# Value products of attention: high and low halves side by side in one stationary tile

## The chip, the cores and the metric

One core of one Trainium2 chip runs the kernel. The metric is device time in microseconds (us). The engines are named as in the profile: PE (TensorE matmul), PEld (its weight load), DVE (VectorE), ACT (ScalarE), POOL (GpSimd), SP (SyncE, which here only issues DMAs).

## The reference, cut to what matters

512 tokens of width 1024 pass through two layers of one block and then through a second block.

- Layer 1: short convolutions beside attention over a memory of 256 rows (4 heads of 64), then a feed-forward part.
- Layer 2: banded attention (12 query heads, 4 value heads of 64, each block of 128 tokens sees itself and the block before) beside memory attention, then a feed-forward part.
- Second block: eight heads of 64 in two groups. Each head adds three attentions, each with its own gate: over compressed blocks, over selected blocks and over a window. With 512 tokens the selected blocks are all the valid ones and the window holds all earlier tokens, so both of these are plain causal attention:

```
p = masked_softmax(q @ k.T * scale, causal)     # branch 0: k_s, v_s; branch 1: k_w, v_w
o = g_c * (p_c @ v_c) + g_s * (p_s @ v_s) + g_w * (p_w @ v_w)
flat = blocks of 32 tokens, stride 16;  k_c, v_c = gelu(flat @ w1) @ w2     # 31 blocks a group
```

Four retention heads, gates and an output projection follow.

## The kernel before, in words

All products are made at nearly full fp32 precision from pieces of a shorter type (`float32r`). A value x is split into hi = round(x) on ACT (`copy`, L65) and lo = x - hi on DVE (`lo_of`, L75, or L71 with a scale). A product is then three matmuls into the same PSUM tile: hi*hi, hi*lo, lo*hi (`mm3`, L111 to L113; `proj_tok`, L133 to L135). Weights come by DMA into `wr`, are split into `wh` and `wl`, and are used once.

In an attention the scores of 128 queries go into a PSUM tile `lg` (`logits`, L234 and L235), DVE subtracts mask and maximum, ACT makes the exponentials and their sum, DVE scales the rows. PE transposes the probabilities 128x128 at a time (L253) into a PSUM tile `tp`, and `split_p` splits these into hi (ACT) and lo (DVE). `pv` then multiplies by the values. A value tile holds, per key block, hi and lo of all heads with 64 zero columns between neighbours, so that a stationary of 128 columns is either [value, 0] or [0, value]. Both heads of a pair thus accumulate into one PSUM tile `po` of 128 rows: even head in rows 0 to 63, odd head in rows 64 to 127. The last key block has only 128 queries; `pv_last` copies these probabilities unsplit and does the product in full fp32 (L279). The compressed attention's product is full fp32 as well (L845).

Per pair of heads: memory attention (`mem_attention`) has 2 key blocks of 512 queries for each head; banded attention (`band_head`) has key blocks 0 to 2 of 256 queries and block 3 of 128; causal attention (`causal_head`, called for 2 branches) has key blocks 0 to 3 of 512, 384, 256 and 128 queries. There are 2 memory pairs in each of two layers, 6 banded pairs, and 4 causal pairs.

`compress` (called for keys and for values) makes flat (62 columns for 31 blocks of 2 groups) and multiplies it with four weight units of 4 x 256 columns, three matmuls of 256 columns for each of 16 pieces (L635 to L637).

Tiles come from pools with a fixed number of buffers for each tag; a tile waits until the buffer that it takes has been read for the last time. The dependences and the order on each engine are worked out when the kernel is built: code is taken in program order, and later work that is ready (projections of the next pair, the next stage) may be put ahead on an engine whose next work is not. Each engine then runs its own list in order. PSUM has `pp`=2, `lg`=3, `tp`=2, `po`=1 buffers of one bank. Probabilities live in `pa` (6 buffers of 512 columns): a causal head takes three, a banded head two.

Of the kernel before, what the change touches and what calls it, by code (L numbers as in the profile page):

```python
# [8 lines left out]
F32 = mybir.dt.float32  # L9
# [14 lines left out]
KWORDS = 2 * 9 * 64  # L24
# [3 lines left out]
class Build:  # L28
# [3 lines left out]
    def __init__(self, ctx, tc, T, out):  # L32
        self.tc, self.nc, self.T, self.out = tc, tc.nc, T, out
        pool = lambda n, b, **k: ctx.enter_context(tc.tile_pool(name=n, bufs=b, **k))
        self.cst = pool("cst", 1)
        self.wp = pool("wp", 1)
        self.wbufs = dict(wr=2, wh=3, wl=3)
        self.sl = pool("sl", 1)
        self.sm = pool("sm", 4)
        self.psp = pool("psp", 1, space=PSUM)  # L40
        self.dr = pool("dr", 1, space=DRAM)
        self.n = 0
        self.bufs = dict(h=16, b=16, t=4, pa=6, pb=10, q=4, v=4, x=8, R=1, s=3, sa=1, k3=2, v3=1)
        self.pbufs = dict(pp=2, lg=3, tp=2, po=1)
# [192 lines left out]
    def value_tile(self):  # L237
        v = self.slot("v", F32R, (128, KWORDS), "v")
        self.nc.gpsimd.memset(v.bitcast(F32), 0.0)
        return v.rearrange("p (s j c) -> p s j c", s=2, c=64)  # L240

    def fill_values(self, v, ps, rs):

        hi, lo = v[:, 0, 1::2], v[:, 1, 1::2]
        src = ps.rearrange("p (h c) -> p h c", c=64)
        self.copy(hi, src, rs)
        self.lo_of(lo, src, hi, rs)
# [20 lines left out]
    def last_value(self, ps, rs):  # L268

        v = self.slot("v3", F32, (128, 576), "v3").rearrange("p (j c) -> p j c", c=64)  # L270
        self.nc.gpsimd.memset(v, 0.0)
        self.copy(v[:, 1::2], ps.rearrange("p (h c) -> p h c", c=64), rs)
        return v

    def pv_last(self, po, v, kv, odd, ps, stop):
        t = self.slot("k3", F32, (128, 128), "k3")
        self.copy(t, ps)
        s = slice(2 * kv, 2 * kv + 2) if odd else slice(2 * kv + 1, 2 * kv + 3)
        self.nc.tensor.matmul(po, v[:, s].rearrange("p j c -> p (j c)"), t, start=False, stop=stop)  # L279
# [6 lines left out]
    def load_consts(self):  # L286
# [3 lines left out]
        self.const("pad", [128, 88])  # L290
        self.ones = self.const("ones", [128, 128])
        nc.vector.memset(self.ones, 1.0)
        self.zero = self.const("zero", [128, 128], F32R)
        self.copy(self.zero, self.ones, 0.0)
# [60 lines left out]
    def mem_kv(self, layer):  # L355
# [11 lines left out]
        def done(tb, ps):  # L367
            hl = [self.slot("b", F32R, name="mv")[:, :384] for _ in range(2)]
            for t in hl:
                nc.gpsimd.memset(t.bitcast(F32), 0.0)  # L370
            hi, lo = (t.rearrange("p (i c) -> p i c", i=2) for t in hl)
            for i in range(2):
                for o in range(2):
                    src = ps[:, 128 * i + 64 * o:128 * i + 64 * o + 64]
                    d = slice(128 * o, 128 * o + 64)
                    self.copy(hi[:, i, d], src, self.mrs[:, tb:tb + 1])
                    self.lo_of(lo[:, i, d], src, hi[:, i, d], self.mrs[:, tb:tb + 1])
            vs.append(hl)
# [4 lines left out]
    def mem_attention(self, qs, ks, vs):  # L383
# [3 lines left out]
        for pair in range(2):  # L387
            po = self.psum("po")
            for odd in range(2):
# [16 lines left out]
                for kb in range(2):  # L406
                    t = self.transposes([(qb * 128, ps_[qb][:, kb * 128:kb * 128 + 128]) for qb in range(4)], 512)
                    th, tl = self.split_p(t)
                    c = 192 * pair + 64 * odd
                    vh, vl = (x[:, c:c + 128] for x in vs[kb])  # L410
                    self.mm3(po, vh, vl, th, tl, odd == 0 and kb == 0, odd == 1 and kb == 1)
            res.append(self.split(po, "b", name="ym"))
# [93 lines left out]
    def layer_b(self):  # L506
# [17 lines left out]
        def done(tb, ps):  # L524
            v = self.value_tile()
            self.fill_values(v, ps, rs[:, tb:tb + 1])
            vs.append(v)
            if tb == 3:
                vs.append(self.last_value(ps, rs[:, 3:]))
# [8 lines left out]
        for pair in range(6):  # L538
            q = self.stack_q(self.queries(T["b_w_q"][pair], h, R))
            bias = self.bias(pair)  # L540
            po = self.psum("po")
            nc.tensor.matmul(po.rearrange("p (a b) -> p a b", a=4), self.zero, self.zero.unsqueeze(1).to_broadcast([128, 4, 128]), start=True, stop=False)
# [8 lines left out]
    def band_head(self, po, hd, odd, q, ks, vs, bias):  # L551
# [21 lines left out]
        cur, prev = (lambda kb: p[kb][:, -128:]), (lambda kb: p[kb + 1][:, :128])  # L573
        tp = self.transposes([(0, cur(0)), (128, prev(0)), (256, cur(1)), (384, prev(1))], 512)
        th, tl = self.split_p(tp)
        for kb in range(2):
            self.pv(po[:, kb * 128:kb * 128 + 256], vs[kb], kv, odd, th[:, kb * 256:kb * 256 + 256], tl[:, kb * 256:kb * 256 + 256], False, False)
        tp = self.transposes([(0, cur(2)), (128, prev(2)), (256, cur(3))], 384)
        th, tl = self.split_p(tp[:, :256])
        self.pv(po[:, 256:], vs[2], kv, odd, th, tl, False, False)  # L580
        self.pv_last(po[:, 384:], vs[4], kv, odd, tp[:, 256:384], odd == 1)
# [30 lines left out]
    def compress(self, kT, j):  # L612
# [14 lines left out]
        fs = [self.split(f.rearrange("p l c -> p (l c)"), "pb", n=496, name="fl") for f in fl]  # L627
        ps = self.psum("pp")[:62, :256]
        mm = nc.tensor.matmul
        for u in range(4):  # L630
            wh, wl = self.weights(T["cmp_w1"][j, u], 4, 256)
            for k in range(4):
                i = 4 * u + k
                a, b = (f[:, 62 * (i % 8):62 * (i % 8) + 62] for f in fs[i // 8])
                mm(ps, a, wh[:, k], start=i == 0, stop=False)  # L635
                mm(ps, b, wh[:, k], start=False, stop=False)
                mm(ps, a, wl[:, k], start=False, stop=i == 15)  # L637
        return ps

    def compress_gelu(self, ps, j):  # L640
# [4 lines left out]
        nc.vector.tensor_copy(x, ps)  # L645
# [30 lines left out]
    def compressed_v(self, hw):  # L676
# [4 lines left out]
        for g in range(2):  # L681
# [7 lines left out]
            for i in range(2):  # L689
                t = self.const(f"vc{g}{i}", [128, 128])  # L690
                nc.vector.memset(t, 0.0)
                for o in range(2):
                    r = slice(64 * i + 32 * o, 64 * i + 32 * o + 32)
                    nc.vector.tensor_copy(t[r, 64 * o:64 * o + 64], ps[r])
# [3 lines left out]
    def cmp_probs(self, g, qpair):  # L698
# [23 lines left out]
        t = self.slot("s", name="pct")  # L722
        self.copy(t, tp)
        return t

    def causal_head(self, po, hd, odd, branch, q, start):
        nc = self.nc
        g = hd // 4
        k = self.nk[branch][g]
        den, nm, r = (self.small(4, name=n) for n in ("den", "nm", "rec"))  # L730
        t = [self.slot("pa", name="p") for _ in range(3)]
        p = [t[0][:, :128], t[1][:, :256], t[0][:, 128:], t[2]]
        for qb in range(4):
            n = 128 * (qb + 1)
# [391 lines left out]
```

## Time and profile before

| | us |
|---|---|
| median of 3 runs | 1671.94 (1670.53 to 1672.93) |
| the profiled execution: its own time | 1670.48 |
| its span, first to last instruction | 1668.7 |
| PE busy | 1634.9 (98%) |
| PEld busy | 1374.2 (82%) |
| DVE busy | 1059.2 (63%) |
| ACT busy | 639.0 (38%) |
| POOL busy | 247.1 (15%) |

Busy time is the union of an engine's instructions. A matmul's row lasts until its result has landed, so rows of neighbouring matmuls overlap; the spacing of their starts is the time that one takes from PE. Parts of the span: memory attention of the first layer lies at about 70 to 100 us, that of the second at 605 to 640, banded attention at 630 to 705, compression at 1120 to 1205, causal attention at 1165 to 1330 us.

### The profile page before, as it was taken

The page shows a single profiled execution, that of the slowest core. Times are in us where ns is not written, and L with a number is a line of the kernel's source. Part 1 is how long each engine was busy: PE and PEld are TensorE (multiplying, and loading weights), DVE is VectorE, ACT ScalarE, POOL GpSimd, SP SyncE. Part 2 cuts the span into 40 slices and gives each one's busy share as a digit, 9 for nine tenths or more (in the row PEclk, how much of TensorE's full clock was granted, in tenths as well). Part 3 has the DMA queues.
Part 4 walks back from the last instruction along what each step waited for, and adds up shares of the span by engine and source line. Part 5 has one row for each costly group of instructions (what it writes and reads, how often), then busy time and mean ns, then how long its engine had stood idle before and what let it go on. Part 6 is the DMA issues. An engine that isn't in the chain of part 4 may idle for free.

```text
span 1668.7 us, 21221 instructions
## 1 busy us (share of the span) xinstructions
PE 1634.9 (98%) x8184; PEld 1374.2 (82%) x8184; DVE 1059.2 (63%) x1828; ACT 639.0 (38%) x1134; POOL 247.1 (15%) x220
## 2 busy tenths in 40 slices
PE   8999999999999999999999999998999999999997
PEld 6888888888888788888888888878788888888887
DVE  7776745444454979875434435588788977764443
ACT  5532333222333467633222223324465533333333
POOL 1111411002011600051100101351001000010010
PEclk9999999999999999999999999999999999999999
DMA  5323222322352422122332332332401122243342
GB/s 188 118 85 102 91 98 91 101 101 85 118 160 91 159 83 84 62 102 88 101 101 95 100 109 91 101 138 93 166 28 58 45 82 83 70 151 114 126 159 88
DMA packets 51557, 171.39 MB, mean 103 GB/s; under 512 B 6680, under 2 KB 6880, under 8 KB 51328
## 3 DMA queue, kind: packets, MB, share of 16 engines
q1 hardware_dynamic: 45504, 151.11, 27.3%
q0 software_dynamic: 5376, 18.82, 3.4%
q8 instruction: 64, 1.05, 0.2%
q14 instruction: 37, 0.30, 0.1%
q10 hardware_dynamic: 576, 0.11, 0.0%
HBM read 160.56 MB, written 11.81 MB: 103 GB/s over the span
## 4 chain that ended last, share of the span: by engine, by line
PE 82%; DVE 10%; issue 2%; ACT 2%; DMA 1%; POOL 1%; DVEq 0%; SPq 0%; ACTq 0%; POOLq 0%
PE pp L112 11%; PE pp L113 11%; PE pp L111 11%; PE lg L111 8%; PE lg L112 8%; PE lg L113 7%; PE tp L112 3%; PE tp L253 2%; PE tp L113 2%; PE tp L111 2%; DVE wl L75 2%; PE po L111 2%; PE po L112 2%; PE po L113 2%; PE pp L133 2%
## 5 line engine op out<-in xcount | busy, mean ns | idle before, releaser
L65 ACT ACTIVATE wh<-wr 128x1024 fp32r<-128x1024 f32 (+2 forms) x280 | 288.5, 1030 | 695.1 <-PE pp L112 228.0
L75 DVE TENSOR_TENSOR wl<-wr,wh 128x1024 fp32r<-128x1024 f32 (+2 forms) x280 | 388.7, 1389 | 55.5 <-ACT wh L65 52.3
L111 PE MATMUL pp<-gh,wh 128*128 128x512 f32 x880 | 348.0, 396 | 7.4 <-ACT wh L65 5.9
L113 PE MATMUL pp<-gh,wl 128*128 128x512 f32 x880 | 347.2, 395 | 0.6 <-DVE wl L75 0.6
L112 PE MATMUL pp<-gl,wh 128*128 128x512 f32 x880 | 346.7, 394 | 0.5 <-DVE gl L71 0.5
L111 PEld LDWEIGHTS pp<-gh,wh 128*128 128x128 f32 x880 | 166.7, 190 | 41.4 <-ACT wh L65 6.4
L113 PEld LDWEIGHTS pp<-gh,wl 128*128 128x128 f32 x880 | 166.4, 189 | 33.9 <-DVE wl L75 1.6
L112 PEld LDWEIGHTS pp<-gl,wh 128*128 128x128 f32 x880 | 166.6, 189 | 33.2 <-DVE gl L71 1.3
L111 PE MATMUL lg<-gh,wh 128*128 128x512 f32 x408 | 159.8, 392 | 0.0
L112 PE MATMUL lg<-gl,wh 128*128 128x512 f32 x408 | 159.1, 390 | 0.0
L113 PE MATMUL lg<-gh,wl 128*128 128x512 f32 x408 | 158.8, 389 | 0.0
L68 POOL TENSOR_TENSOR u<-u,z 128x512 f32<-128x512 f32 x44 | 64.8, 1472 | 549.7 <-DVE u L68 432.6
L68 DVE TENSOR_TENSOR u<-lg,Rf 128x512 f32<-128x512 f32 x44 | 30.4, 691 | 137.4 <-PE lg L113 137.3
L112 PEld LDWEIGHTS lg<-gl,wh 128*128 128x128 f32 x408 | 76.7, 188 | 16.5 <-issue 0.7
L111 PEld LDWEIGHTS lg<-gh,wh 128*128 128x128 f32 x408 | 76.6, 188 | 16.3 <-issue 0.5
L113 PEld LDWEIGHTS lg<-gh,wl 128*128 128x128 f32 x408 | 76.6, 188 | 16.1 <-issue 0.2
L112 PE MATMUL tp<-actl,wh 128*128 128x512 f32 x216 | 84.5, 391 | 0.9 <-DVE actl L75 0.9
L111 PE MATMUL tp<-acth,wh 128*128 128x512 f32 x216 | 84.1, 389 | 0.0
L113 PE MATMUL tp<-acth,wl 128*128 128x512 f32 x216 | 84.1, 389 | 0.0
L68 DVE TENSOR_TENSOR z<-pp,Rf 128x512 f32<-128x512 f32 x44 | 30.4, 691 | 69.5 <-PE pp L113 65.7
L504 DVE TENSOR_TENSOR x<-x,tp 128x512 f32<-128x512 f32 x36 | 24.6, 683 | 65.5 <-PE tp L113 65.5
L71 DVE SCALAR_TENSOR_TENSOR gl<-x,gains,gh 128x512 fp32r<-128x512 f32 x40 | 52.9, 1338 | 0.5 <-ACT gh L65 0.5
(422 smaller groups left out, 3088.9 us busy)
## 6 DMA issues: line engine op xcount, KB each, us to landing
wr<-in_w_gate_dram SPq DMA_DIRECT2D x44, 512.0 KB, 3.2
wr<-in_w_up_dram SPq DMA_DIRECT2D x44, 512.0 KB, 3.2
wr<-in_w_in_dram SPq DMA_DIRECT2D x44, 512.0 KB, 3.2
wr<-in_w_down_dram SPq DMA_DIRECT2D x32, 448.0 KB, 3.3
wr<-in_a_w_in_dram SPq DMA_DIRECT2D x18, 512.0 KB, 3.2
wr<-in_w_down_dram SPq DMA_DIRECT2D x16, 512.0 KB, 3.5
wr<-in_a_w_out_dram SPq DMA_DIRECT2D x8, 512.0 KB, 3.2
wr<-in_b_w_q_dram SPq DMA_DIRECT2D x8, 512.0 KB, 3.2
```

The costliest lines, as they stand in the source:

```text
L65: self.nc.scalar.activation(out, in_, AF.Copy, scale=scale)
L68: (eng or self.nc.vector).tensor_tensor(out, a, b, op=ALU.mult)
L71: (eng or self.nc.vector).scalar_tensor_tensor(out, a, s, b, op0=op0, op1=op1)
L75: self.nc.vector.tensor_tensor(out, x, hi.bitcast(F32), op=ALU.subtract)
L111: mm(ps, ah, bh, start=start, stop=False)
L112: mm(ps, ah, bl, start=False, stop=False)
L113: mm(ps, al, bh, start=False, stop=stop)
L133: mm(ps, a, wh, start=k == 0, stop=False)
L253: self.nc.tensor.transpose(ps[:, c:c + 128], src, self.ident)
L504: nc.vector.tensor_tensor(self.x[c], self.x[c], ps, op=ALU.add)
```

## The change

A value tile now holds, per head, 64 columns of hi and beside them 64 columns of lo, with no zeros; it is the stationary [hi | lo] of one matmul. The moving operand is the split probabilities: one pass with hi, one with lo, where there were three. The result has 128 rows for one head: rows 0 to 63 belong to hi of the values, 64 to 127 to lo, and `heads_out` adds the two halves (ACT copies the lower rows to SBUF, DVE adds) for each head of the pair. `po` becomes a tile of 1024 columns (two banks), and `lg` goes from three buffers to two.

- Memory attention: two matmuls of 512 columns in place of three for each head and key block.
- Banded attention: the softmax of both heads of a pair comes first (`band_probs`), then the products of both (`band_values`): two matmuls of 256 for each of 4 key blocks; the last block's 128 queries are padded with 128 zero columns (POOL). The matmul with zeros that opened `po` goes.
- Causal attention: both heads of a pair share keys and values, so their queries are put into one moving operand (`causal_pair`): 8 matmuls of 512 and 4 of 256 columns for a pair and a branch. Probabilities of a pair take five `pa` buffers. The branch is now the outer loop, the head the inner one.
- Compressed attention: four matmuls of 256 for each head, on split probabilities.
- Compression: flat's hi (62 columns) and lo (62 columns, from column 64) become one stationary, so two matmuls for each piece in place of three; `compress_gelu` adds the two halves.

```
-        self.bufs = dict(..., R=1, s=3, sa=1, k3=2, v3=1)
-        self.pbufs = dict(pp=2, lg=3, tp=2, po=1)
+        self.bufs = dict(..., R=1, s=4, sa=1)
+        self.pbufs = dict(pp=2, lg=2, tp=2, po=1)
...
-    def pv(self, po, v, kv, odd, th, tl, start, stop):
-        s = slice(2 * kv, 2 * kv + 2) if odd else slice(2 * kv + 1, 2 * kv + 3)
-        vh, vl = (v[:, i, s].rearrange("p j c -> p (j c)") for i in range(2))
-        self.mm3(po, vh, vl, th, tl, start, stop)
+    def pv(self, po, v, t, start, stop):
+        for i in range(2):
+            self.nc.tensor.matmul(po, v, t[i], start=start and i == 0, stop=stop and i == 1)
+    def heads_out(self, po, out, form=lambda a: a):
+        for o in range(2):
+            t = self.slot("s", name="half")[:64]
+            self.copy(form(t), po[o][64:])
+            self.nc.vector.tensor_tensor(form(out[64 * o:64 * o + 64]), po[o][:64], form(t), op=ALU.add)
...
 layer_b, for each pair:
-            for odd in range(2):
-                self.band_head(po, 2 * pair + odd, odd, q[odd], ks, vs, bias[:, odd])
-            ys.append(self.split(po, "b", name="y"))
+            probs = [self.band_probs(2 * pair + odd, q[odd], ks, bias[:, odd]) for odd in range(2)]
+            y = self.slot("t", name="yb")
+            po = self.band_values(pair, probs, vs)
+            self.heads_out([po[:, :512], po[:, 512:]], y)
+            ys.append(self.split(y, "b", name="y"))
...
+    def causal_pair(self, po, pair, branch, q):
+        mid = self.slot("pa", name="p")
+        for odd in range(2):
+            t = [self.slot("pa", name="p") for _ in range(2)]
+            p = [t[0][:, :128], mid[:, 256 * odd:256 * odd + 256], t[0][:, 128:], t[1]]
...            (scores, exponentials and scaling as in causal_head)
+        for kb, qbs in ((0, (0, 1)), (0, (2, 3)), (1, (2, 3)), (2, (2, 3))):
+            t = self.split_p(self.transposes(block(kb, qbs), 512))
+            self.pv(view[:, qbs[0] // 2], values[kb], [two(a) for a in t], branch == 0 and kb == 0, False)
+        t = self.split_p(self.transposes(block(1, (1,)) + [(256 + c, x) for c, x in block(3, (3,))], 512))
+        for i, kb in enumerate((1, 3)):
+            self.pv(view[:, i, :, 128:], values[kb], [two(a[:, 256 * i:256 * i + 256]) for a in t], False, False)
...
 compress:
-                mm(ps, a, wh[:, k], start=i == 0, stop=False)
-                mm(ps, b, wh[:, k], start=False, stop=False)
-                mm(ps, a, wl[:, k], start=False, stop=i == 15)
+                mm(ps, fs[u][:, k], wh[:, k], start=i == 0, stop=False)
+                mm(ps, fs[u][:, k], wl[:, k], start=False, stop=i == 15)
```

## Rows read from the trace of the kernel before

**Rows 1.** The page: engines' busy time; the chain that ended last.
```profile
PE 1634.9 (98%) x8184; PEld 1374.2 (82%) x8184; DVE 1059.2 (63%) x1828; ACT 639.0 (38%) x1134; POOL 247.1 (15%) x220
...
PE 82%; DVE 10%; issue 2%; ACT 2%; DMA 1%; POOL 1%; DVEq 0%; SPq 0%; ACTq 0%; POOLq 0%
```
**Rows 2.** Windows: stretch, length, busy us and instructions of each engine, clock, DMA.
```profile
core 0: us, PE busy (x) PEld busy (x) DVE busy (x) ACT busy (x) POOL busy (x), PEclk, DMA share, GB/s
60.00:80.00 20.00, 19.85 (x110) 17.18 (x110) 14.51 (x29) 12.88 (x31) 0.00 (x0) 0.97 0.32 107
80.00:100.00 20.00, 19.98 (x109) 16.35 (x108) 16.67 (x40) 11.77 (x35) 0.00 (x0) 1.00 0.29 93
...
620.00:640.00 20.00, 19.98 (x109) 16.23 (x107) 18.43 (x54) 14.61 (x42) 0.71 (x1) 1.00 0.13 41
640.00:660.00 20.00, 19.78 (x129) 17.07 (x128) 17.99 (x58) 14.26 (x42) 0.71 (x1) 1.00 0.28 93
660.00:680.00 20.00, 19.98 (x122) 16.80 (x121) 18.53 (x60) 15.18 (x46) 0.71 (x1) 1.00 0.24 70
680.00:700.00 20.00, 19.96 (x126) 16.96 (x126) 18.33 (x65) 14.50 (x47) 0.00 (x0) 1.00 0.22 76
...
1160.00:1180.00 20.00, 15.93 (x88) 13.64 (x89) 14.76 (x34) 12.04 (x22) 1.38 (x1) 0.91 0.47 153
...
1220.00:1240.00 20.00, 20.00 (x122) 16.95 (x121) 17.49 (x56) 13.34 (x37) 0.00 (x0) 1.00 0.00 1
1240.00:1260.00 20.00, 19.90 (x115) 16.87 (x114) 17.54 (x49) 11.71 (x33) 1.29 (x1) 1.00 0.15 53
1260.00:1280.00 20.00, 19.32 (x93) 15.10 (x93) 17.82 (x49) 11.99 (x31) 3.73 (x4) 1.00 0.21 67
1280.00:1300.00 20.00, 19.90 (x127) 17.09 (x126) 17.75 (x56) 12.10 (x36) 0.00 (x0) 1.00 0.09 27
1300.00:1320.00 20.00, 19.30 (x113) 15.92 (x112) 19.50 (x61) 14.62 (x42) 1.26 (x1) 1.00 0.01 2
```
**Rows 3.** Timeline of PE in causal attention: start, length, instruction.
```profile
1233.21 1.12 PE L845 MATMUL po<-pct,vc 128*128 128x512 f32 x2
1233.77 0.80 PE L235 MATMUL lg<-kl,q 128*128 128x512 f32 x1
...
1234.88 0.40 PE L111 MATMUL pp<-gh,wh 128*128 128x512 f32 x1
1235.11 0.39 PE L112 MATMUL pp<-gl,wh 128*128 128x512 f32 x1
```
**Rows 4.** Timeline in banded attention, at the end of one head's value products.
```profile
665.27 0.28 PE L113 MATMUL po<-tph,v 128*128 128x256 f32 x1
665.39 0.28 PE L111 MATMUL po<-tp,v 128*128 128x256 f32 x1
...
665.75 0.39 PE L279 MATMUL po<-k,v 128*128 128x128 f32 x2
665.89 0.48 PE L111 MATMUL pp<-gh,wh 128*128 128x512 f32 x1
```
**Rows 5.** Groups of DVE by shape, 600 to 712 us: busy, mean ns, idle before.
```profile
L75 DVE TENSOR_TENSOR tpl<-tp,tph 128x512 fp32r<-128x512 f32 x20 | 13.6, 687 | 1.9 <-ACT tph L65 1.8
...
L210 DVE TENSOR_TENSOR q<-qs,q 64x512 fp32r<-64x512 f32 x16 | 11.0, 686 | 0.8 <-ACT q L65 0.3
...
L75 DVE TENSOR_TENSOR tp<-tp,tp 128x256 fp32r<-128x256 f32 x12 | 5.0, 419 | 0.7 <-ACT tp L65 0.5
```
**Rows 6.** Groups of DVE by shape, 1205 to 1335 us.
```profile
L738 DVE CUSTOM_DVE_ANT_0 p<-lg,causal 128x512 f32<-128x512 f32 x14 | 9.5, 679 | 0.0
L75 DVE TENSOR_TENSOR tpl<-tp,tph 128x384 fp32r<-128x384 f32 x16 | 8.8, 548 | 1.0 <-ACT tph L65 0.9
```
**Rows 7.** Groups of ACT by shape, 1205 to 1335 us.
```profile
L739 ACT ACTIVATE p<-p,nm 128x512 f32<-128x512 f32 x14 | 10.0, 718 | 1.7 <-DVE nm L738 1.7
L65 ACT ACTIVATE tph<-tp 128x512 fp32r<-128x512 f32 x16 | 9.5, 592 | 9.7 <-PE tp L253 9.7
```
**Rows 8.** The chain that ended last, in compression alone (1140 to 1205 us).
```profile
by line: DVE wl L75 16.4%; PE pp L113 9.2%; PE pp L111 8.8%; PE pp L112 8.4%; DMA wr<-in_cmp_w_dram 7.6%; DVE flat L626 5.5%; DMA wr<-in_w_in_dram 5.4%; issue 4.1%; DVE kl L220 4.1%; ACT wh L65 3.3%; PE pp L637 2.6%; DVE v L71 2.5%; DVE rb 
```

More of the change, by code (lines that the diff above doesn't have):

```diff
@@ L23 @@
 WMAX = 1152
-KWORDS = 2 * 9 * 64
+KWORDS = 1024
 FFG = [(0, 8), (8, 15), (15, 22)]
@@ L367, in done @@
         def done(tb, ps):
[L368 to L378, printed above, removed]
+            vs.append(self.fill_values(ps, self.mrs[:, tb:tb + 1], "b"))
         self.proj_tok(T["w_mem_v"][layer], gm, 256, 2, done, tag=("tp",) if layer else ("lg",))
@@ L407, in mem_attention @@
                     t = self.transposes([(qb * 128, ps_[qb][:, kb * 128:kb * 128 + 128]) for qb in range(4)], 512)
[L408 to L412, printed above, removed]
+                    self.pv(po[:, 512 * odd:512 * odd + 512], vs[kb][:, h], self.split_p(t), kb == 0, kb == 1)
+            y = self.slot("t", name="ym")
+            self.heads_out([po[:, :512], po[:, 512:]], y)
+            res.append(self.split(y, "b", name="ym"))
         return res
@@ L688, in compressed_v @@
             two = []
[L689 to L694, printed above, removed]
+            for hd in range(4):
+                t = self.const(f"vc{g}{hd}", [128, 128], F32R)
+                nc.vector.memset(t.bitcast(F32), 0.0)
+                r = slice(32 * hd, 32 * hd + 32)
+                self.copy(t[r, :64], ps[r])
+                self.lo_of(t[r, 64:], ps[r], t[r, :64])
                 two.append(t)
@@ L721, in cmp_probs @@
         tp = self.transposes([(qb * 128, p[:, qb].rearrange("p h c -> p (h c)")) for qb in range(4)], 512)
[L722 to L726, printed above, removed]
+        return self.split(tp, "pb", name="pct")
+    def causal_pair(self, po, pair, branch, q):
         nc = self.nc
-        g = hd // 4
+        g = pair // 2
         k = self.nk[branch][g]
[L730 to L734, printed above, removed]
-            w = max(n, 256)
-            lg = self.psum("lg")
-            self.logits(lg[:, :w], q[:, qb * 128:qb * 128 + 128], [a[:, :w] for a in k])
-            nc.vector.tensor_tensor_reduce(p[qb], lg[:, :n], self.causal[:, 512 - n:], -1.0, 1.0e30, ALU.add, ALU.min, nm[:, qb:qb + 1])
-            nc.scalar.activation(p[qb], p[qb], AF.Exp, bias=nm[:, qb:qb + 1], scale=-1.0, accum_out=den[:, qb:qb + 1])
-        nc.vector.reciprocal(r, den)
-        self.mul(r, r, self.gates[:, :, hd * 3 + 1 + branch])
-        for qb in range(4):
-            self.scaled(p[qb], r[:, qb:qb + 1])
-        for kb in range(3):
-            parts = [((qb - kb) * 128, p[qb][:, kb * 128:kb * 128 + 128]) for qb in range(kb, 4)]
-            if kb == 2:
-                parts.append((512 - kb * 128, p[3][:, 384:]))
-            tp = self.transposes(parts, 0)
-            th, tl = self.split_p(tp[:, :512 - kb * 128])
-            self.pv(po[:, kb * 128:], self.nv[kb], 2 * branch + g, odd, th, tl, start and kb == 0, False)
-            if kb == 2:
-                self.pv_last(po[:, 384:], self.nv[4], 2 * branch + g, odd, tp[:, 512 - kb * 128:640 - kb * 128], False)
@@ new lines, in causal_pair @@
+        mid = self.slot("pa", name="p")
+        probs = []
+        for odd in range(2):
+            hd = 2 * pair + odd
+            den, nm, r = (self.small(4, name=n) for n in ("den", "nm", "rec"))
+            t = [self.slot("pa", name="p") for _ in range(2)]
+            p = [t[0][:, :128], mid[:, 256 * odd:256 * odd + 256], t[0][:, 128:], t[1]]
+            for qb in range(4):
+                n = 128 * (qb + 1)
+                w = max(n, 256)
+                lg = self.psum("lg")
+                self.logits(lg[:, :w], q[odd][:, qb * 128:qb * 128 + 128], [a[:, :w] for a in k])
+                nc.vector.tensor_tensor_reduce(p[qb], lg[:, :n], self.causal[:, 512 - n:], -1.0, 1.0e30, ALU.add, ALU.min, nm[:, qb:qb + 1])
+                nc.scalar.activation(p[qb], p[qb], AF.Exp, bias=nm[:, qb:qb + 1], scale=-1.0, accum_out=den[:, qb:qb + 1])
+            nc.vector.reciprocal(r, den)
+            self.mul(r, r, self.gates[:, :, hd * 3 + 1 + branch])
+            for qb in range(4):
+                self.scaled(p[qb], r[:, qb:qb + 1])
+            probs.append(p)
```

123 lines of the change are left out of this document (67 added, 56 removed).

## The prediction

> **What bounds the kernel now.** I read the page first. PE is busy for 98% of the span and carries 82% of the chain that ended last [rows 1]; DVE has 10% of the chain and 63% busy time. Taken alone this says that each PE microsecond removed is a microsecond of time. But a matmul's row runs on until its result has landed, so the busy share of PE cannot show how much room it has, and the share of DVE is an average over stages. So I read the windows of the stages that the change touches [rows 2]. The reader is to see two things there. In banded attention DVE is busy 18.43, 17.99, 18.53 and 18.33 us of 20: 73.3 of 80, 92%. In causal attention it is 17.49 to 19.50 of 20: 90.1 of 100. So in the two stages where most of the removed matmuls lie, a second engine is almost as full as PE. The fullest slice of all, 19.50 of 20, shows how far DVE can be packed in this kind of work: 97.5%. In memory attention of the first layer DVE has room (14.51 and 16.67 of 20). In compression even PE is not full (15.93 of 20, granted clock 0.91 of full speed), and the chain there is mostly the split of weights on DVE and the weights' DMAs [rows 8].
>
> The Trainium skill has a rule on just this (Perfetto Trace Analysis, Identifying the Most-Contended Engine): matmul busy time is no good measure of how near TensorE is to its limit, and the weight-load share should be read in its place, while for VectorE the busy share is fair. The windows agree as far as they go: by that rule banded attention has PE at 81 to 85% and DVE at 90 to 93%, so DVE is the most contended engine there, and the removal of matmuls by itself would give nothing in that stage. The sum below would stand without this rule.
>
> **What PE loses.** The cost of a matmul is the spacing of starts: 0.23 us for 512 columns (1234.88 to 1235.11) [rows 3], 0.12 us for 256 (665.27 to 665.39) and 0.14 us for the pair of records of one full fp32 product of 128 columns (665.75 to 665.89) [rows 4]. The full fp32 product of 512 columns takes 0.56 us (1233.21 to 1233.77) [rows 3]. For 384 columns I take the middle of 0.12 and 0.23, 0.175.
> - Memory attention: 2 layers x 2 pairs x 2 heads x 2 key blocks = 16 products lose one matmul of 512: 16 x 0.23 = 3.7 us, half of it in each layer.
> - Banded: before, a head has 9 x 0.12 + 0.14 + half of the opening matmul 0.115 = 1.34 us; after, 8 x 0.12 = 0.96. Saved 0.38 x 12 heads = 4.5 us.
> - Causal: before, a head and branch has 3 x (0.23 + 0.175 + 0.12) + 0.14 = 1.72 us; after, a pair and branch has 8 x 0.23 + 4 x 0.12 = 2.32, 1.16 for a head. Saved 0.56 x 16 = 8.9 us. The compressed product goes from 0.56 to 8 x 0.12 = 0.96 a pair: 4 x 0.4 = 1.6 us back. Net 7.3 us.
> - Compression: 32 pieces lose one matmul of 256: 3.8 us.
>
> The transposes stay as many as they were. In all PE has 19.3 us less.
>
> **What DVE gains.** `heads_out` is not in the trace. Its DVE half reads 64 rows by 512 columns; the nearest row is the 64x512 subtraction of `stack_q`, 0.69 us [rows 5], so 1.38 us a pair. From below, 0 is excluded, since the add is a new pass over 512 columns; 0.60 each is what overlap with a neighbour could make of it.
> - Banded: the splits of transposed probabilities go from 2 x (0.69 + 0.42) = 2.22 us a pair to 3 x 0.69 + 0.42 = 2.49 [rows 5]; with `heads_out` 1.65 us a pair, 9.9 us for 6 pairs (8.8 by the lower price).
> - Causal: a pair and branch goes from 2 x (0.69 + 0.55 + 0.42) = 3.32 us [rows 5, 6] to 5 x 0.69 = 3.45: 8 x 0.13 = 1.0 us; `heads_out` 4 x 1.38 = 5.5; the compressed probabilities are now split, 2 x 0.69 = 1.4. Together 7.9 us.
> - Memory: 2 pairs x 1.38 = 2.8 us in each layer.
>
> ACT gains a copy of about 0.59 us [rows 7] for each head in `heads_out` and loses the small copies of `pv_last`; at 14.3 to 15.2 us of 20 in banded attention [rows 2] it has room, so I cost it at nothing; without that room it would be 6 x 2 x 0.59 = 7 us less the copies saved. The zero fills on POOL (0.71 us of 20 busy in those windows) are hidden likewise; they stand behind the loads of bias tables on POOL's queue, which come one pair ahead.
>
> **The sum, stage by stage.**
> - Memory, first layer: DVE has 8.8 us free in 40 and needs 2.8; PE is the limit, -1.8 us.
> - Memory, second layer: its end lies in the slice with DVE at 18.43; PE -1.8 against DVE +2.8, I take 0.
> - Banded: DVE has 73.3 + 9.9 = 83.2 us to do where the stage had 80. Packed as in the fullest slice (97.5%) this takes 85.3 us: +5.3. If every idle microsecond were used it would be +3.2; at today's 92%, +10.8. What is late is the last pair's result, and behind it the output projection of the layer, which needs all pairs. I take +5.3: PE has less to do, so DVE waits less for it.
> - Causal: 90.1 + 7.9 = 98.0 us in 100. At 97.5% this is 100.5, +0.5; at today's 90%, 108.8, +8.8; if PE alone decided, -7.3. I take +2, near the first, since PE hands back 7.3 us of the same stage.
> - Compression: the chain there is weights; I take -1 of the 3.8 us (bounds -3.8 and +1 for four smaller splits in place of two and a new half to add).
> - `lg` with two buffers: its reader on DVE is what a score matmul waits for, and two buffers still let one be filled while the other is read: 0, at most +2.
>
> Sum: -1.8 + 0 + 5.3 + 2 - 1 + 0 = +4.5 us. On the profiled execution's own 1670.48 us (its span of 1668.7 and 1.8 around it) this is 1675.0; the median of the runs lies 1.5 us above that execution, so I predict 1676.5 us, slower by 0.3%. This case has a range of its own from 1669 (all free DVE time used, causal -1, compression -3) to 1684 (both stages at today's density in part). About 0.2%, 3.3 us, is what a measurement of this kernel can tell from no change.
>
> **The rivals.**
> 1. *PE alone decides* (faster). For it: PE's share of the chain is 82% [rows 1], and PE is above 19.3 us of 20 in all attention windows [rows 2]. Against it: DVE's idle time in banded attention is 6.7 us of 80, and the change brings 9.9. It decides if DVE's idle time turns out to be waiting for PE, and the weight splits that stand in the banded windows for the next stage can be done later. Then memory -3.7, banded -4.5 to 0, causal -7.3, compression -1 to -3.8: -12 to -19, so 1653 to 1660 us. Chance 0.30.
> 2. *The softmax of the next branch can't start* (slower by more). A causal pair holds five of the six `pa` buffers until the last group of its transposes, where before two heads of three buffers took turns. Between the last maximum and the first split probabilities lies a chain of exponential 0.72 [rows 7], scaling about 0.5 and the copy of the transposed block 0.59 [rows 7], some 1.8 us; the next branch's 0.68 us passes [rows 6] no longer cover it. Eight pair-branches: up to 14 us. Work of projections and rotary tables may fill the gap; it decides if less than half is filled. Then +7 to +14 on top of the forecast: 1684 to 1691. Chance 0.13.
> 3. *An even trade*: what PE hands back in memory, causal and compression is what banded attention costs, within 3.3 us of 1671.94. Chance 0.15.
>
> **Numbers.** The forecast's case has 0.42, of which I put 0.08 inside 0.2%. Slower: 0.34 + 0.13 + 0.01 = 0.48; same: 0.08 + 0.11 = 0.19; faster: 0.30 + 0.03 = 0.33. The range from 1655 to 1690 leaves out the best end of rival 1 and the worst of rival 2, less than 2 in 10.
>
> **What would show it.** After the change the windows of banded attention should have DVE at 19 us of 20 or more, with the stage about 5 us longer; the additions of `heads_out` should be rows of 64x512 at 0.6 to 0.7 us; causal attention should be of nearly the same length with DVE above 18 of 20. Matmuls into `po` in attention should sum to about two thirds. I am wrong if banded attention gets shorter, or if DVE's idle time there stays at 8% while the stage shrinks with PE; if the causal windows show DVE idle before the first splits of each branch, rival 2 holds.

## The result and the profile after

The changed kernel takes 1724.59 us (median of 4 runs, 1722.7 to 1728.18), the old one beside it 1671.24 (1667.79 to 1672.93). The ratio is 1.0324, with an interval of [1.03, 1.0349]: 53 us slower. The forecast had the sign right (1676.5 us), but 53 us lie outside its range, which ended at 1690.

The page of the changed kernel, busy time and the chain that ended last, against [rows 1]:

```profile
PE 1648.7 (96%) x8038; PEld 1366.7 (79%) x8038; DVE 1079.8 (63%) x1846; ACT 655.8 (38%) x1125; POOL 243.4 (14%) x222
...
PE 79%; DVE 13%; issue 3%; ACT 3%; POOL 1%; DMA 1%; DVEq 0%; ACTq 0%; SPq 0%; POOLq 0%
```

PE runs 146 matmuls fewer and is busy for longer (1648.7 us against 1634.9). DVE's busy time grew by 20.6 us, near the forecast's 9.9 + 7.9 + 2 x 2.8 = 23.4. So no engine got 53 us of new work (that PE is busy for longer with fewer matmuls lies in part at its clock, see the last section). The windows tell where the time went (columns as in [rows 2]):

```profile
60.00:80.00 20.00, 19.83 (x110) 16.86 (x109) 14.32 (x26) 10.80 (x24) 0.00 (x0) 1.00 0.28 98
80.00:100.00 20.00, 20.00 (x109) 16.37 (x108) 18.68 (x40) 14.41 (x37) 0.52 (x1) 1.00 0.35 113
...
640.00:660.00 20.00, 16.95 (x94) 12.81 (x93) 16.83 (x57) 14.21 (x42) 1.27 (x3) 1.00 0.22 66
660.00:680.00 20.00, 16.50 (x81) 12.41 (x80) 15.85 (x48) 12.89 (x31) 1.26 (x3) 0.91 0.21 67
680.00:700.00 20.00, 16.31 (x81) 12.32 (x81) 15.47 (x42) 11.54 (x31) 1.28 (x3) 0.91 0.17 49
700.00:720.00 20.00, 13.99 (x77) 10.45 (x78) 14.26 (x42) 11.48 (x31) 1.82 (x5) 1.00 0.18 58
720.00:740.00 20.00, 19.33 (x97) 15.46 (x96) 12.71 (x39) 10.02 (x29) 0.00 (x0) 0.92 0.09 27
...
1260.00:1280.00 20.00, 19.02 (x101) 14.76 (x100) 17.63 (x47) 13.17 (x32) 0.00 (x0) 1.00 0.10 37
1280.00:1300.00 20.00, 15.82 (x64) 10.38 (x63) 12.37 (x35) 8.73 (x21) 0.66 (x1) 0.83 0.06 18
1300.00:1320.00 20.00, 20.00 (x90) 16.33 (x90) 19.16 (x51) 11.66 (x28) 3.45 (x5) 0.91 0.23 72
1320.00:1340.00 20.00, 18.46 (x90) 13.82 (x89) 16.33 (x46) 11.02 (x27) 0.00 (x0) 0.86 0.14 47
1340.00:1360.00 20.00, 18.43 (x98) 14.12 (x97) 17.45 (x55) 13.07 (x35) 0.00 (x0) 0.97 0.01 2
1360.00:1380.00 20.00, 14.51 (x65) 10.62 (x64) 12.12 (x26) 6.65 (x12) 2.44 (x2) 0.80 0.08 26
```

In banded attention (640 to 740 us) PE and DVE have become idle together: DVE is busy for 14.3 to 16.8 us of 20 in the first four slices, where it was 18.0 to 18.5 in the three slices of this stage [rows 2], and PE for 14.0 to 17.0, where it was 19.8 and more. Causal attention shows the same in two slices. When two engines that were both full are idle at once, each may be waiting for the other in turn, and the thing to look for is a wait that comes once per iteration. From the list of waits in the banded stretch of the changed kernel, 640 to 740 us (engine, line, releaser; us in total, times, longest):

```profile
DVE yb L270 <- ACT half L66: 10.5, 7, 2.0
...
PE pp L112 <- DVE qs L72: 10.0, 5, 2.0
ACT half L66 <- PE po L263: 9.5, 6, 2.2
POOL bias L325 <- DVE yb L270: 8.8, 3, 3.0
```

and PE's only wait in the same stage of the kernel before (620 to 715 us):

```profile
PE lg L234 <- DVE q L210: 0.2, 1, 0.2
```

`qs` are the scaled queries of the *next* pair, `bias` its table of biases. The end of the third pair in the timeline of the changed kernel:

```profile
684.00 0.59 ACT L66 ACTIVATE half<-po 64x512 f32<-64x512 f32 x1 [1.30 <-PE po L263]
684.63 0.68 DVE L270 TENSOR_TENSOR yb<-po,half 64x512 f32<-64x512 f32 x1 [1.48 <-ACT half L66]
685.24 0.67 DVE L72 SCALAR_TENSOR_TENSOR qs<-pp,Rb 128x512 f32<-128x512 f32 x1
...
685.97 0.80 PE L112 MATMUL pp<-gh,wh 128*128 128x512 f32 x1 [2.00 <-DVE qs L72]
685.97 0.69 DVE L270 TENSOR_TENSOR yb<-po,half 64x512 f32<-64x512 f32 x1
...
686.96 0.71 POOL L325 DMA_DIRECT2D bias<-band  x1 [2.96 <-DVE yb L270]
...
687.41 0.63 PE L112 MATMUL pp<-gh,wh 128*128 128x512 f32 x1
687.84 0.63 PE L113 MATMUL pp<-gl,wh 128*128 128x512 f32 x1
...
689.34 0.35 DVE L537 CUSTOM_DVE_ANT_0 p<-lg,bias,negsink 128x128 f32<-128x128 f32 x1 [0.60 <-PE lg L236]
```

The pair's products end, ACT copies the lower half, DVE adds, and only then does DVE scale the next pair's queries; PE stood idle for 2.00 us until that was done. The next softmax begins at 689.34, 4.7 us after the first addition. In the old kernel such work was interleaved: the split of the fourth result, the softmax of the next pair and the queries of the last pair follow one another on DVE.

```profile
685.89 0.69 DVE L75 TENSOR_TENSOR yl<-po,yh 128x512 fp32r<-128x512 f32 x1
...
686.57 0.48 DVE L564 CUSTOM_DVE_ANT_0 p<-lg,bias,negsink 128x256 f32<-128x256 f32 x1
...
688.24 0.68 DVE L71 SCALAR_TENSOR_TENSOR qs<-pp,Rb 128x512 f32<-128x512 f32 x1
```

In the changed kernel `qs` starts 0.6 us behind the first addition at the end of each of the five banded pairs that have a next one (`qs` at 651.57, 667.64, 685.24, 702.72 and 718.87 us). Where tags `t` and `s` are freed (experiment `e_both` below) it does not: there the last pair's queries are scaled before even the fourth pair's result is added (additions at 689.58 and 691.38, shown further below).

```profile
687.95 0.68 DVE L72 SCALAR_TENSOR_TENSOR qs<-pp,Rb 128x512 f32<-128x512 f32 x1
```

In the program's text `yb` takes its buffer of tag `t` before the next pair's `qs` takes its own, and in the trace `qs` stands directly behind the first instruction that writes `yb`. The result of a pair is the last thing that the pair makes, so nothing of the next pair's queries comes before it. That is the theory: tags `t` and `s` are handed out in the program's order, and `heads_out`'s two new tiles put the pairs one behind the other. Its rivals: too few buffers; `lg` with two; `pa` too small; DVE's additional work.

To follow the runs I use three marks in each trace: the first instruction that writes `Rb` (layer 2 begins), the first that writes `R2` (second block begins; the profile, which leaves numbers out, calls it `R`), and the end of the first low split of the merged result `mgl`. In us, each row from one execution:

```
              to Rb    Rb to R2    R2 to mgl   mgl to end   (span)
before        583.8      535.5       371.6        177.8     1668.7
after         580.5      566.8       396.1        177.5     1720.9
e_own         582.1      572.8       381.3        177.7     1713.9
e_half        579.5      570.2       394.9        177.7     1722.3
e_both        580.7      542.7       379.3        177.8     1680.5
e_ahead       582.2      550.7       395.2        177.7     1705.8
e_t5          582.8      568.6       394.5        177.6     1723.4
e_noadd       583.3      535.4       369.3        177.6     1665.6
e_dve         582.8      542.1       372.4        177.7     1675.1
b_stage_t     584.1      548.9       371.6        177.6     1682.2
b_stage_own   584.8      534.9       371.3        177.7     1668.7
b_mem         584.2      532.9       371.5        177.7     1666.3
b_cmp         584.2      534.5       373.0        177.8     1669.5
```

The change costs 31.3 us in the stretch with memory and banded attention and 24.5 us in the one with compression and causal attention; up to `Rb` it is 3.3 us ahead.

### The profile page after: what moved, and what is told of

It reads as the page before. It is cut to its first block, busy times and chain, and to the rows that moved or that the text cites. A ratio compares the mean times of both kernels' runs of the same rounds, so it can differ in the third digit from the quotient of the medians.

```text
span 1720.9 us, 20990 instructions
## 1 busy us (share of the span) xinstructions
PE 1648.7 (96%) x8038; PEld 1366.7 (79%) x8038; DVE 1079.8 (63%) x1846; ACT 655.8 (38%) x1125; POOL 243.4 (14%) x222
## 3 DMA queue, kind: packets, MB, share of 16 engines
q8 instruction: 63, 1.03, 0.2%
## 4 chain that ended last, share of the span: by engine, by line
PE 79%; DVE 13%; issue 3%; ACT 3%; POOL 1%; DMA 1%; DVEq 0%; ACTq 0%; SPq 0%; POOLq 0%
PE pp L112 11%; PE pp L113 11%; PE pp L114 11%; PE lg L112 7%; PE lg L113 7%; PE lg L114 7%; PE po L263 3%; PE tp L113 2%; PE tp L114 2%; PE tp L112 2%; DVE wl L76 2%; PE tp L250 2%; DVE gl L72 1%; PE pp L134 1%; PE pp L135 1%
## 5 line engine op out<-in xcount | busy, mean ns | idle before, releaser
L250 PE MATMUL tp<-ident,p 128*128 128x128 f32 x308 | 58.5, 291 | 3.9 <-DVE p L274 3.4
```

The costliest lines, as they stand in the source:

```text
L250: self.nc.tensor.transpose(ps[:, c:c + 128], src, self.ident)
```

## The experiments

Of each change only the lines that matter are shown.

**Tiles of `heads_out` in other tags.** `e_both` takes `y` from `sa` (free at that time) and `half` from a tag of its own; `e_own` does the first alone, `e_half` the second.

```
-        self.bufs = dict(..., s=4, sa=1)
+        self.bufs = dict(..., s=3, sa=1, hf=1)
-            t = self.slot("s", name="half")[:64]
+            t = self.slot("hf", name="half")[:64]
-            y = self.slot("t", name="yb")          (and ym, yo)
+            y = self.slot("sa", name="yb")
```

> The changed kernel with buffers of their own for the two tiles that heads_out brought: its result y (out of tag t, where the next pair's scaled queries live) and its copied half (out of tag s, where the next pair's bias table and rotary tiles live). Same arithmetic. Theory A: a tag hands out its buffers in program order, so the next pair's queries and bias wait for heads_out of this pair, and that is the lost time: banded attention back from 102 us to 72 to 80 us, whole kernel 1665 to 1690 us. Theory B, the forecast's (DVE is simply full): no gain, since DVE's work is the same; 1720 us. Theory C (two lg buffers instead of three): 1720 us. Theory D (five of six pa buffers held by a causal pair): banded recovers, causal stays about 22 us longer, 1690 to 1700 us.

> The changed kernel with y alone moved out of tag t (half stays in s). Theory A: the queries come early, but the bias table still waits for half, so banded attention gains little, 0 to 10 us; causal attention, which needs no bias, gains some: 1700 to 1720 us. If y alone is the cause: 1665 to 1690. B and C: 1725 us.

> The changed kernel with half alone moved out of tag s (y stays in t). Theory A: the bias comes early but the queries still wait for y, little gain in banded attention, 1705 to 1725 us. If half alone is the cause: 1665 to 1690. B and C: 1725 us.

`e_both` measured 1682.4 us, 1.0077 [1.0054, 1.01] of before; `e_own` 1715.33 us, 1.0262 [1.0247, 1.0277]; `e_half` 1728.5 us, 1.0339 [1.0319, 1.0359]. Together the two moves give back 42 us, alone 9 us and nothing. The table shows why. In causal attention tag `t` decides: `e_own` already has 381.3 us there, against 396.1. In banded attention either tag is enough to keep the pairs apart (572.8 and 570.2 us), and only both moves bring 542.7. In `e_own` PE no longer waits for `qs` there; it waits 13.6 us, in four waits, for the split of the pair's result. With both moves DVE is at 19 of 20 in two of the banded windows, as the prediction had drawn them; in the first below it is at 18.35, and PE at 15.39 with a clock of 0.91:

```profile
640.00:660.00 20.00, 15.39 (x86) 12.03 (x85) 18.35 (x58) 13.64 (x42) 1.29 (x3) 0.91 0.13 40
660.00:680.00 20.00, 19.76 (x109) 15.85 (x108) 19.17 (x56) 15.06 (x38) 1.84 (x5) 1.00 0.44 145
680.00:700.00 20.00, 19.98 (x120) 16.58 (x119) 19.25 (x59) 14.13 (x40) 0.56 (x2) 1.00 0.17 53
```

**The order, or the number of buffers?** `e_t5` gives tag `t` a fifth buffer and changes nothing else (a tile that is never used makes the room). `e_ahead` keeps the tags and their sizes; in the banded stage it takes the next pair's tiles before this pair's result.

```
+        ahead = lambda i: (self.stack_q(self.queries(T["b_w_q"][i], h, R)), self.bias(i))
+        q, bias = ahead(0)
         for pair in range(6):
-            q = self.stack_q(self.queries(T["b_w_q"][pair], h, R))
-            bias = self.bias(pair)
             probs = ...
+            if pair < 5:
+                q, bias = ahead(pair + 1)
             y = self.slot("t", name="yb")
```

> The changed kernel with five buffers in tag t in place of four (the room comes from an unused pad tile). Nothing else is changed. If too few buffers hold the next pair's queries back: up to 20 us faster than the changed kernel's 1724.6 us. If it is the order in which the tag is handed out, more buffers change nothing: 1720 to 1728 us.

> The changed kernel with its tags and their sizes as they are; in the banded stage alone, the next pair's query tile (tag t) and bias table (tag s) are taken in the program before this pair's result and half. If the order of taking is the cause: the stretch from the start of layer 2's norm row to that of the second block goes from 566.8 us to 541 to 545 (542.7 with tags of their own), the whole to 1698 to 1704 us; causal attention stays as slow as it is. If it is the number of buffers: no change, 1720 to 1728 us.

`e_t5`: 1725.36 us, 1.0324 [1.0302, 1.0346], as slow as the change. `e_ahead`: 1707.3 us, 1.0214 [1.0197, 1.0231]. For tag `t` the number is not the cause. With five buffers the causal stretch, where this tag alone decides, stays at 394.5 us, and in banded attention `qs` still stands directly behind the first addition of each pair; the third pair:

```profile
688.40 0.68 DVE L270 TENSOR_TENSOR yb<-po,half 64x512 f32<-64x512 f32 x1 [1.49 <-ACT half L66]
689.01 0.67 DVE L72 SCALAR_TENSOR_TENSOR qs<-pp,Rb 128x512 f32<-128x512 f32 x1
```

That the banded stretch as a whole is no shorter proves less, since tag `s` was left as it was and holds the pairs apart by itself; a further buffer of `s` was not run. The order is a cause: without another buffer the stretch Rb to R2 falls from 566.8 to 550.7 us, and causal attention, which this run leaves alone, stays at 395.2. I had expected 541 to 545; 8 us against own tags remain, and which tile holds them back I did not try. The Trainium skill (Perfetto Trace Analysis, Optimization Strategy) says that a gap that repeats on the engine that should be full can mean that there is no room for the next tile, and names buffer count and tile sizes. The gap did repeat here, five times 2.0 us on PE between 640 and 740 us; with the fifth buffer of `t` it is there five times 2.0 us as well.

**The same order put into the old kernel.** The old kernel's banded result goes through one copy on DVE into a tile of tag `t` (`b_stage_t`) or of `sa` (`b_stage_own`) before it is split. Nothing else of the change is there.

```
-            ys.append(self.split(po, "b", name="y"))
+            y = self.slot("t", name="yb")          (b_stage_own: "sa")
+            nc.vector.tensor_copy(y, po)
+            ys.append(self.split(y, "b", name="y"))
```

> The kernel before (old products, three lg buffers, old po), with one thing added in banded attention: the finished po of a pair is copied by DVE into a tile y out of tag t, and y is split in place of po. Six more DVE instructions of about 0.7 us, 4 us of work. Theory A (buffers of a tag are handed out in program order, so the next pair's queries wait for this pair's y): banded attention goes from 72 us to 90 us or more, the kernel to 1685 to 1705 us. Theory B (work on DVE): +4 us at most, 1674.

> The same as b_stage_t with y out of tag sa, which nothing else uses in this stage. Same instructions. Both theories: 0 to +5 us, 1670 to 1676 us; the difference to b_stage_t is the tag's order alone.

`b_stage_t`: 1684.17 us, 1.0082 [1.0063, 1.0101], just under the range expected; `b_stage_own`: 1671.21 us, 1.0002 [0.9992, 1.0011]. The two differ in one word. Six copies of 0.69 us on DVE cost nothing that shows; the tag costs 13 us, all of it in Rb to R2 (548.9 against 534.9). The fifth pair's copy and the last pair's queries on DVE, with tag `t` and with `sa`:

```profile
709.45 0.69 DVE L546 COPY yb<-po 128x512 f32<-128x512 f32 x1 [1.20 <-PE po L279]
710.06 0.68 DVE L71 SCALAR_TENSOR_TENSOR qs<-pp,Rb 128x512 f32<-128x512 f32 x1
```
```profile
687.82 0.66 DVE L71 SCALAR_TENSOR_TENSOR qs<-pp,Rb 128x512 f32<-128x512 f32 x1
...
698.43 0.68 DVE L546 COPY yb<-po 128x512 f32<-128x512 f32 x1
```

With `t` the queries follow the copy by 0.6 us, as in the changed kernel; with `sa` they come 10.6 us before it.

**`lg` and `pa`.** `b_lg2` is the old kernel with two `lg` buffers; `e_pa7` is `e_both` with seven `pa` buffers.

```
-        self.pbufs = dict(pp=2, lg=3, tp=2, po=1)
+        self.pbufs = dict(pp=2, lg=2, tp=2, po=1)     (b_lg2)
-        self.bufs = dict(..., pa=6, ...)
+        self.bufs = dict(..., pa=7, ...)              (e_pa7)
```

> The kernel before with two lg buffers in place of three, nothing else. Theory A: within 0.5% of before, 1665 to 1680 us. Theory C: most of the 53 us, 1700 us or more.

> e_both with seven pa buffers in place of six (the unused pad tile is left out to make room). Theory D: a causal pair's five buffers no longer keep the next branch's softmax out, and causal attention, which takes 17 us longer than before in e_both, gives back 5 to 15 us: 1668 to 1678 us. Theory B: 1680 to 1684 us.

`b_lg2`: 1671.28 us, 1.0002 [0.9991, 1.0012]. `e_pa7`: 1684.03 us, 1.008 [1.0065, 1.0096], not faster than `e_both`. Neither buffer count costs anything that shows.

**The 12 us that `e_both` still loses.** `e_noadd` is `e_both` without the low half: one copy by ACT of the upper rows, no addition. `e_dve` makes that copy on DVE. `e_pool` keeps both halves, with two copies by ACT and the addition on POOL. `e_late` places a banded pair's `heads_out` behind the next pair's softmax.

```
-            self.copy(form(t), po[o][64:])
-            self.nc.vector.tensor_tensor(form(out[64 * o:64 * o + 64]), po[o][:64], form(t), op=ALU.add)
+            self.copy(form(out[64 * o:64 * o + 64]), po[o][:64])                          (e_noadd)
+            self.nc.vector.tensor_copy(form(out[64 * o:64 * o + 64]), po[o][:64])         (e_dve)
...
+            self.copy(form(out[me]), po[o][:64])                                          (e_pool)
+            self.nc.gpsimd.tensor_tensor(form(out[me]), form(out[me]), form(t), op=ALU.add)
...
             probs = ...
+            if pair:
+                finish(po)                            (e_late: heads_out and split of the pair before)
             po = self.band_values(pair, probs, vs)
```

> The changed kernel with the tag order undone (1682.4 us), and heads_out cut to one copy by ScalarE of the upper 64 rows of each head: left out are the copy of the lower rows and VectorE's addition, so the low half of the values is lost. 28 additions of about 0.68 us and as many links of the chain copy, addition, split are gone. If these are the remaining 12 us: 1660 to 1672 us. If the pairing of the heads and the other edits make it: 1678 to 1682 us.

> The run without additions (1666.0 us: upper 64 rows copied by ScalarE alone, low half of the values left out) with that copy made by VectorE in place of ScalarE: 28 passes of 64x512 on VectorE again, some 0.68 us each, but one link in the chain as there and not two. If VectorE's time is what the additions cost: 1678 to 1684 us. If it is the chain from ScalarE's copy to the addition, with VectorE's queue waiting behind it: 1664 to 1670 us.

> e_both with the add of the two halves taken off DVE: ACT copies both halves, POOL adds them (28 DVE instructions of 0.69 us less, 19 us; 28 more ACT copies of 0.59 us, 17 us). Theory B for what is left of the loss (12 us): DVE is the limit in banded and causal attention, so this gains 6 to 14 us: 1668 to 1676 us. Theory D (pa buffers): no gain, 1680 to 1686.

> The changed kernel with the tag order undone (1682.4 us), and in the banded stage heads_out of a pair is placed in the program after the softmax of the next pair, so that VectorE has other work while ScalarE copies. Nothing is left out. If the chain copy, addition holds VectorE's queue up: the stage goes from 78.4 us to 73 or 74, the whole to 1676 to 1679 us. If it is VectorE's time, or if work is already put ahead there: 1681 to 1684 us.

`e_noadd`: 1665.97 us, 0.9978 [0.9967, 0.9989]; `e_dve`: 1676.15, 1.0029 [1.0017, 1.0042]; `e_pool`: 1689.54, 1.0114 [1.0098, 1.0131]; `e_late`: 1682.93, 1.0076 [1.0061, 1.0091]. `e_dve` came out between its two expectations, and `e_pool` above both of its own. So `heads_out` costs 16.4 us (1682.4 - 1666.0): 10.2 when the one pass per head goes from ACT to DVE, another 6.2 when a copy by ACT comes before it (by the ratios, each to the old kernel beside it, 8.5 and 8.0). The first is a matter of DVE, whose pass costs the same whether it copies or adds; the groups of the banded stage in `e_dve` and in the changed kernel:

```profile
L268 DVE COPY yb<-po 64x512 f32<-64x512 f32 x12 | 8.2, 681 | 1.3 <-PE po L263 1.1
```
```profile
L270 DVE TENSOR_TENSOR yb<-po,half 64x512 f32<-64x512 f32 x12 | 8.2, 684 | 10.8 <-ACT half L66 10.5
```

and the banded stretch is as slow in `e_dve` as in `e_both` (542.1 and 542.7 us). In that stretch `e_noadd` has 535.4. The second lies in the causal stretch (372.4 against 379.3); whether it is ACT's time or the longer chain the runs don't separate. `e_late` moves nothing: in `e_both` the next pair's softmax already stands between the two additions of a pair, as its timeline of DVE shows:

```profile
689.58 0.68 DVE L270 TENSOR_TENSOR yb<-po,half 64x512 f32<-64x512 f32 x1 [0.21 <-ACT half L66]
...
690.87 0.48 DVE L537 CUSTOM_DVE_ANT_0 p<-lg,bias,negsink 128x256 f32<-128x256 f32 x1
...
691.38 0.68 DVE L270 TENSOR_TENSOR yb<-po,half 64x512 f32<-64x512 f32 x1
```

On POOL one addition takes twice as long (1.42 against 0.68 us), and there is one more copy by ACT before it:

```profile
L272 POOL TENSOR_TENSOR yb<-yb,half 64x512 f32<-64x512 f32 x12 | 17.1, 1424 | 49.4 <-ACT yb L66 46.6 <-DVE nm L539 2.8
```

**Parts of the change in the old kernel.** `b_mem` has the two-pass products in memory attention alone (result in `sa`, and two `lg` buffers, since `po` takes two banks), `b_cmp` the wide compression products alone, `b_order` only the order "softmax of both heads, then the products of both" of the banded stage with the old products; `b_memord` is `b_mem` and `b_order` together.

```
-                    self.mm3(po, vh, vl, th, tl, odd == 0 and kb == 0, odd == 1 and kb == 1)
+                    self.pv2(po[:, 512 * odd:512 * odd + 512], vs[kb][:, h], self.split_p(t), kb == 0, kb == 1)
...
-                mm(ps, a, wh[:, k], start=i == 0, stop=False)
-                mm(ps, b, wh[:, k], start=False, stop=False)
-                mm(ps, a, wl[:, k], start=False, stop=i == 15)
+                mm(ps, fs[u][:, k], wh[:, k], start=i == 0, stop=False)
+                mm(ps, fs[u][:, k], wl[:, k], start=False, stop=i == 15)
...
+            probs = [self.band_probs(2 * pair + odd, q[odd], ks, bias[:, odd]) for odd in range(2)]
             for odd in range(2):
-                self.band_head(po, 2 * pair + odd, odd, q[odd], ks, vs, bias[:, odd])
+                self.band_values(po, 2 * pair + odd, odd, probs[odd], vs)
```

> The kernel before with the change in the memory attention alone: values as 64 high beside 64 low columns, two passes, halves added, the sum in a tag that nothing else waits for. In the changed kernel the first layer came 3.3 us earlier, the second about 5 us later. If the first carries to the end and the second's loss was that of the tag order: 1665 to 1670 us. If the second layer loses by its added work too: 1670 to 1675 us.

> The kernel before with the change in the compression alone: windows split into 62 high beside 62 low columns, two passes by 128 columns in place of three, halves added. TensorE has 3.8 us less to do; in the changed kernel the stage took as long as before, since weights or the windows bound it. That theory: 1669 to 1673 us, no change. If TensorE bounds it: 1667 to 1669 us.

> The kernel before with one thing of the change: in the banded stage the softmax of both heads of a pair is issued first, then the transposes and old products of both heads. With the tag order undone, the changed kernel still loses about 6 us in the banded stage (78.4 us from the end of memory 2 to the last pair's result, against 72.5 of before). If that is the pairing of the heads (TensorE waits for both softmaxes): 1675 to 1680 us. If it is the chain of copy and addition behind each pair, this kernel has it not: within 0.2% of before, 1668 to 1674 us.

> The kernel before with two passes in the memory attention and the softmax of both heads first in the banded stage. Apart they measured 0.9992 and 0.9991 of before, both within the uncertainty. If both are real: 1665 to 1668 us, ratio 0.998; if both are chance: within 0.1% of before.

`b_mem`: 1668.12 us, 0.9992 [0.9983, 1.0001]; `b_cmp`: 1672.01, 1.0013 [1.0004, 1.0022]; `b_order`: 1668.02, 0.9991 [0.9981, 1.0001]; `b_memord`: 1670.71, 1.0004 [0.9995, 1.0013]. The pairing of the heads costs nothing that shows. The two that came out a little low don't add up, so no complete version here beats the old kernel by an amount that can be measured. `e_noadd`, which leaves the addition out, comes nearest to showing what the removed matmuls alone bring: 3.7 us of the 19.3, with the one copy by ACT and the other edits still in it.

## Why the prediction was right in sign and wrong in size

**The step that failed** is the costing of `heads_out` in "What DVE gains" and in the sum: 1.38 us of DVE for a pair, ACT's copy at nothing, and "what is late is the last pair's result". It priced the new instructions, and the price was right: 0.684 us measured for 0.69. It did not ask from which tag the two new tiles are taken and who takes the next buffer of it. That is 42 us of the 53. Once this is undone the stage sum is near in one stretch and not in the other: in `e_both` Rb to R2 is 7.2 us longer (forecast 0 for memory and +5.3 for the band), R2 to mgl 7.7 us (forecast +2 and -1). The whole, 12.2 us slower than the old kernel beside it, is still more than twice the forecast's 4.5. So the sign came out right for a reason that holds in part, while most of the slowdown has another one.

- *DVE bounds banded attention*: wrong for the changed kernel as it is, where DVE is at 71 to 84% in the four windows, in `e_both` right for two windows (19.17 and 19.25 of 20) and not for the one before them (18.35).
- *Causal +2*, with compression's -1: 7.7 us in place of +1. `b_cmp`, with the compression alone, has the stretch 1.4 us longer, and `e_dve` 0.8 us, so DVE's share was about right. `e_both` has 6.9 us more than `e_dve`: that is the copy by ACT that I costed at nothing, with the chain that hangs on it. Nor did causal attention stay "of nearly the same length": in `e_both` its last result comes 228.7 us after `R2`, before 210.5; of these 18 us, 7.7 are left at `mgl`.
- *Memory of the first layer, -1.8*: the changed kernel does reach `Rb` 3.3 us earlier, but only in part through its products. PE's granted clock at 40 to 80 us differs between executions (column before the DMA share); before, 40 to 60 us, with the slice after it in [rows 2]; then the changed kernel, with its next slice above; then `b_mem`:

```profile
40.00:60.00 20.00, 16.83 (x102) 15.36 (x101) 14.41 (x33) 6.94 (x11) 8.25 (x7) 0.94 0.35 117
```
```profile
40.00:60.00 20.00, 17.33 (x110) 15.30 (x109) 14.39 (x33) 8.26 (x13) 5.55 (x3) 1.00 0.41 131
```
```profile
40.00:60.00 20.00, 17.11 (x98) 14.83 (x97) 14.29 (x32) 6.54 (x9) 7.18 (x3) 0.96 0.32 111
60.00:80.00 20.00, 19.83 (x111) 17.37 (x111) 12.99 (x23) 11.29 (x24) 0.00 (x0) 0.96 0.33 113
```

  The clock that was missing before is 0.06 x 20 + 0.03 x 20 = 1.8 us, an upper estimate of its part in the 3.3. `b_mem` has the same products at nearly the old clock (0.96 and 0.96, before 0.94 and 0.97) and comes to `Rb` at 584.2 us, 0.4 later than before; `e_ahead`, at 0.94 and 0.97, comes at 582.2, 1.6 earlier. The term lies between 0 and -1.6, and single executions don't tell more.
- *Compression -1*: `b_cmp` shows no gain, if anything some 2 us of loss; the forecast's reason, a chain of weights, fits this, but no run tests it.
- *`lg` with two buffers, 0*: right (`b_lg2`).
- *Rival 1, PE alone decides*: refuted. Without additions the change gains 3.7 us, not 12 to 19, and nothing in the stretch with banded attention (535.4 us against 535.5).
- *Rival 2, the next iteration can't start*: near in effect, wrong in place. Iterations were put one behind the other, but by tags `t` and `s`, in the banded stage too; a seventh buffer of `pa`, which I had named, gives nothing back.
- *Rival 3, an even trade*: not reached, not even by `e_both` (12.2 us slower).

## What to carry to other kernels

A new temporary costs more than its instructions: look up which pool tag it is taken from, what else takes from that tag, and what the next iteration takes first. If a tile that is written at the end of an iteration shares a tag with one that starts the next, overlap between iterations is gone, and a further buffer need not help; a tag of its own, or taking the next iteration's tile earlier, does. In this trace it showed as two formerly full engines idle at once, with a wait that comes once per iteration on the next iteration's first tile.

## What was not expected of the hardware

Short idle times of PE can cost twice. Windows around the end of that third pair in the changed kernel (2 us without a matmul, then projections into `pp`, then the softmax running again):

```profile
684.00:686.00 2.00, 0.03 (x1) 0.04 (x1) 1.31 (x3) 1.24 (x3) 0.00 (x1) 0.93 0.00 0
686.00:688.50 2.50, 2.50 (x6) 2.02 (x7) 2.44 (x4) 1.84 (x3) 0.71 (x1) 0.50 0.10 13
689.40:691.00 1.60, 1.60 (x10) 1.34 (x9) 0.73 (x5) 1.01 (x4) 0.00 (x0) 1.00 0.05 21
```

After the idle time the granted clock is 0.50, which is the lower of its two levels, 1.2 GHz; the matmuls of 512 columns then start 0.43 us apart (687.41 to 687.84 in the timeline above), against 0.23 at full clock [rows 3]. The Trainium skill (TensorE: Matmul & The Clock Gate, Back-to-back issue gap) gives formulas for the gap of an isolated matmul, which come to about 427 ns for 512 columns at the lower and 216 ns at the higher level, and 131 ns measured in a stream at the higher. The trace agrees with the first within 0.01 us and is 0.01 us above the second; 131 ns is not seen. Not every such gap has this price: of the five waits of 2.0 us for `qs` between 640 and 740 us, those that end at 652.3 and 703.5 leave the clock at 1.00 (windows 640 to 660 and 700 to 720).

Over the windows shown, the missing clock adds up to 0.26 x 20 = 5.2 us in banded (640 to 740) and 0.63 x 20 = 12.6 us in causal attention (1260 to 1380), where the old kernel had 1.00 in the slices of [rows 2] at 620 to 700 and 1220 to 1320. Over the whole span the mean granted clock is 0.983 of 1720.9 us, before 0.995 of 1668.7: 29.3 us against 8.3 are missing. The difference, 21 us, is an upper estimate of what the clock added to the 53 us, since PE was also waiting for some of that time; the forecast had nothing for it. In `e_both` the mean is 0.992 of 1680.5 us, 13.4 us missing, so up to 16 us of what it gives back is clock.
